# A row-variance kernel: the last row stored as four 128 B lines straight from the transpose, without closing barriers

## The chip, the cores and the metric

The kernel runs on one core of a Trainium2 chip. The metric is the device time of one execution in microseconds; lower is better. Positions in a trace are microseconds from the start of its span.

## The reference

```python
x = np.random.randn(8192, 8192).astype(np.float32)
def reference(x):
    return np.var(x, axis=1)        # 8192 variances
```

The input is 268 MB, the output 32 KB.

## The kernel before

SyncE streams the rows through three buffers; VectorE sums, ScalarE squares. The last two blocks are cut into pieces with a semaphore each, so that little work is left when the last one lands. What matters here is the end. The variances of the last 128 rows (called a row below, as they are one row of 128 outputs) come out of an aggregate as one column, are transposed in blocks of 32 x 32, and then lie as four lines of 32 values on partitions 0, 32, 64 and 96:

```python
        def variances(j, *marks):
            wait(v, *marks)
            ok = V.mark(v.bn_aggr(out=mv[j][:, 0:2], in_=st[j]))
            wait(v, ok)
            return V.mark(v.transpose(vl[j][:, 0:32], mv[j][:, 1:33]))
        ...
        ok = variances(1, done[1]["B"], done[1]["A"])
        wait(g, (V.sem, V.n - 1))
        g.sem_clear(range(own[0].num, own[-1].num + 1))
        final = []
        for b, (eng, copy) in enumerate(((v, v.tensor_copy), (a, a.copy), (g, g.tensor_copy)), 1):
            wait(eng, ok)
            moved = copy(out=vl[1][0:1, b * 32 : b * 32 + 32], in_=vl[1][b * 32 : b * 32 + 1, 0:32])
            final.append(moved.then_inc(gathered, 1).ins)
        ...                                                        # cut: three earlier stores
        final.append(store(out_r[r + 1 : r + 2], vl[1][0:1, :], (gathered, 3)).ins)
        sp.wait_ge(gathered, 3).then_inc(gathered, -3)
    tc.close()
    tc.compile()
    nc.sync.wait_ge(stored, 64).then_inc(stored, -64)
    ...                                                            # cut: closing barriers moved early
```

Three engines copy one line each beside the first, so that the row leaves as one line of 512 B. Two closing barriers of all engines and GpSimd's clear of the semaphores follow. The row before it, ready earlier, already leaves as four lines of 128 B.

## Time and profile before

| | before |
|---|---|
| time, median of the first four executions | 626.74 us (626.65 to 627.13) |
| span of the profiled execution | 625.66 us |
| share of the span in which the load queue is busy | 99.5% |
| last transpose starts | 624.057 |
| store of the last row issued | 624.572 to 624.799 |
| its semaphore complete, end of SyncE's wait | 625.629, 625.662 |

Read it from the end: the span ends with SyncE's wait for the last store. Everything from the transpose to there is one chain of 1.605 us; before the transpose VectorE works from 618.59 on with no pause over 35 ns, taking the last pieces about as they land; up to there the loads alone set the pace.

### The profile page before, as it was taken

Reading aid. Unit: us, or ns where it says so; the run is one execution under the profiler, and the core shown is the slowest. Engines: PE = TensorE matmul, PEld = TensorE weight load, DVE = VectorE, ACT = ScalarE, POOL = GpSimd, SP = SyncE. Lnnn points to the kernel's source line nnn. Section 1 sums busy time; section 2 is a strip of 40 time slices with the busy share of each in tenths; the row PEclk is TensorE's granted clock in tenths of the full one; section 3 lists DMA queues with packets and bytes.
Section 4 is the critical chain, followed back from the end, with each engine's and each line's share of the span. In section 5 each row is a group of like instructions: output and inputs, shape, how many; then the busy total and the mean of one; then the engine's idle time right before and its main releaser. Section 6 shows DMA issues by size and latency. Waiting matters only on the chain. (4 is left out here: it accounts for less than half of the span.)

```text
span 625.7 us, 990 instructions
## 1 busy us (share of the span) xinstructions
PE 0.6 (0%) x2; PEld 0.2 (0%) x2; DVE 292.1 (47%) x214; ACT 460.4 (74%) x166; POOL 1.6 (0%) x16
## 2 busy tenths in 40 slices
PE   0000000000000000000000000000000000000000
PEld 0000000000000000000000000000000000000000
DVE  0533455334554335543355533555334554345668
ACT  0566886668866688666796667976668866688698
POOL 0000000000000000000000000000000000000000
DMA  9999999999999999999999999999999999999997
GB/s 402 465 406 461 411 402 469 402 469 402 469 402 465 406 457 415 448 423 427 444 406 465 402 469 402 469 402 469 402 465 406 448 423 427 444 406 465 402 421 319
DMA packets 6121, 268.48 MB, mean 429 GB/s; under 512 B 712, under 2 KB 872, under 8 KB 1384
## 3 DMA queue, kind: packets, MB, share of 16 engines
q1 hardware_dynamic: 6120, 268.47, 99.5%
q14 instruction: 1, 0.01, 0.0%
HBM read 268.44 MB, written 0.03 MB: 429 GB/s over the span
## 5 line engine op out<-in xcount | busy, mean ns | idle before, releaser
L176 ACT ACTIVATE junk_a<-rows,means 128x8192 fp8e4 x30 | 213.7, 7122 | 160.7 <-ACTq L174 160.7
L100 DVE CUSTOM_DVE_ANT_0 junk_p<-rows 128x512 f32<-128x512 f32 (+4 forms) x63 | 145.8, 2314 | 325.8 <-DMA rows<-in_x_dram 325.8
L176 ACT ACTIVATE rows<-rows,means x30 | 213.2, 7106 | 0.0
L100 DVE CUSTOM_DVE_ANT_0 junk_s<-rows 128x4096 fp8e4<-128x4096 f32 (+3 forms) x34 | 139.1, 4093 | 5.5 <-DMA rows<-in_x_dram 5.5
L100 DVE DVE_READ_ACCUMULATOR2_ANT means<- 128x1 f32 x90 | 10.9, 121 | 0.0
L241 DVE BATCH_NORM_STATS2 st<-rows 128x6 f32<-128x512 f32 (+1 forms) x14 | 8.7, 672 | 1.0 <-DMA rows<-in_x_dram 1.0
L108 ACT ACTIVATE rows<-rows,st 128x3584 f32<-128x3584 f32 (+3 forms) x4 | 8.9, 2231 | 0.2 <-DVE st L100 0.2
L157 ACT ACTIVATE over<-means x30 | 8.4, 279 | 0.0
L108 ACT ACTIVATE rows<-rows,tmp 128x8192 f32<-128x8192 f32 x1 | 7.1, 7122 | 0.3 <-issue 0.3
L108 ACT ACTIVATE junk_a<-rows,tmp 128x8192 fp8e4<-128x8192 f32 x1 | 7.1, 7108 | 0.0
L176 ACT ACTIVATION_READ_ACCUMULATOR rows<-rows,means x30 | 5.6, 186 | 0.0
L176 ACT ACTIVATION_READ_ACCUMULATOR junk_a<-rows,means x30 | 5.6, 186 | 0.0
L169 ACT ACT_TABLE_LOAD x1 | 1.3, 1283 | 1.9 <-SPq L124 1.9
L214 POOL TENSOR_TENSOR ssq<-ssq,over 128x30 f32<-128x30 f32 x1 | 0.3, 251 | 596.3 <-ACT over L157 596.3
L221 PE MATMUL junk_p<-ident,ssq 128*31 128x128 f32 x2 | 0.6, 422 | 614.4 <-POOL ssq L216 614.4
L268 ACT COPY vl<-vl 1x32 f32<-1x32 f32 x1 | 0.2, 215 | 1.0 <-DVE vl L249 1.0
L247 DVE BATCH_NORM_AGGREGATE mv<-st 128x2 f32<-128x57 f32 (+1 forms) x2 | 0.7, 371 | 0.0
L108 ACT ACTIVATION_READ_ACCUMULATOR rows<-rows,st 128x1 f32 x4 | 0.8, 188 | 0.0
L249 DVE STREAM_TRANSPOSE vl<-mv 128x32 f32<-128x32 f32 x2 | 0.4, 211 | 0.1
L100 DVE DVE_READ_ACCUMULATOR2_ANT st<- 128x1 f32 x4 | 0.4, 112 | 0.0
L258 DVE TENSOR_SCALAR vs<-junk_p 31x256 f32<-31x256 f32 x1 | 0.4, 372 | 0.0
L221 PEld LDWEIGHTS junk_p<-ident,ssq 128*31 128x31 f32 x2 | 0.2, 140 | 614.4 <-POOL ssq L216 614.4
(17 smaller groups left out, 3.2 us busy)
## 6 DMA issues: line engine op xcount, KB each, us to landing
rows<-in_x_dram SPq DMA_DIRECT2D x2, 4096.0 KB, 37.4
rows<-in_x_dram SPq DMA_DIRECT2D x2, 1280.0 KB, 16.0
rows<-in_x_dram SPq DMA_DIRECT2D x1, 1792.0 KB, 11.9
rows<-in_x_dram SPq DMA_DIRECT2D x1, 1088.0 KB, 11.0
rows<-in_x_dram SPq DMA_DIRECT2D x1, 1024.0 KB, 25.5
rows<-in_x_dram SPq DMA_DIRECT2D x2, 512.0 KB, 12.3
rows<-in_x_dram SPq DMA_DIRECT2D x2, 256.0 KB, 13.1
rows<-in_x_dram SPq DMA_DIRECT2D x30, 42.3
```

What stands on the lines that cost most here:

```text
L100: ins = nc.vector.tensor_tensor_reduce(out=junk, in0=src[:, 0 : w // 2], in1=src[:, w // 2 : w], scale=scale, scalar=0.0, op0=ALU.add, op1 ...
L108: return A.mark(nc.scalar.activation(out=src if out is None else out, in_=src, func=ACTF.Square, bias=mean, scale=-1.0, accum_out=acc, **p ...
L157: return a.activation(out=out, in_=k, func=ACTF.Square, bias=rest, scale=root * (K / m - 1.0))
L169: a.activation(out=tmp[:, 7:8], in_=tmp[:, 6:7], func=ACTF.Square)
L176: a.activation(out=row if j else junk_a, in_=row, func=ACTF.Square, bias=about, scale=-1.0, accum_out=ssq[:, bass.ds(i * (J * SLOTS) + s * ...
L214: g.tensor_tensor(out=loop_rows, in0=loop_rows, in1=over[:, 0:t], op=ALU.subtract)
L221: t_ok = T.mark(nc.tensor.transpose(vp[:, j], ssq[:, j : r : J], ident))
L241: ok = V.mark(v.bn_stats(out=st[j][:, b : b + 6], in_=src[:, at : min(at + F, w)]))
L247: ok = V.mark(v.bn_aggr(out=mv[j][:, 0:2], in_=st[j]))
L249: return V.mark(v.transpose(vl[j][:, 0:32], mv[j][:, 1:33]))
L258: vs_ok = V.mark(v.tensor_scalar(out=vs.rearrange("t p j -> t j p"), in0=vp, scalar1=1.0 / m, scalar2=None, op0=ALU.mult))
L268: moved = copy(out=vl[1][0:1, b * 32 : b * 32 + 32], in_=vl[1][b * 32 : b * 32 + 1, 0:32])
```

## The change

Its intent: drop three copies and a wait from the chain, and drop the barriers. The core of the diff (the block that moved the barrier's instructions is cut):

```diff
-        wait(g, (V.sem, V.n - 1))
-        g.sem_clear(range(own[0].num, own[-1].num + 1))
-        for b, (eng, copy) in enumerate(((v, v.tensor_copy), (a, a.copy), (g, g.tensor_copy)), 1):
-            wait(eng, ok)
-            moved = copy(out=vl[1][0:1, b * 32 : b * 32 + 32], in_=vl[1][b * 32 : b * 32 + 1, 0:32])
-            final.append(moved.then_inc(gathered, 1).ins)
+        def lines_of(r):
+            return out_r[r].rearrange("(b k) -> b k", k=32)
-        final.append(store(out_r[r + 1 : r + 2], vl[1][0:1, :], (gathered, 3)).ins)
-        sp.wait_ge(gathered, 3).then_inc(gathered, -3)
+        store(lines_of(r + 1), vl[1][0::32, 0:32], ok)
...
+    for blk in (leave, end):
+        blk.instructions = [i for i in blk.instructions if isinstance(i, mybir.InstUnconditionalBranch)]
+    sp.sem_clear(range(own[0].num, section[0]["range_last"] + 1))
+    sp.wait_ge(stored, 64).then_inc(stored, -64)
```

More of the change, by code (lines that the diff above doesn't have):

```diff
@@ L77 @@
     vp = junk_p[0 : NT - 1, H - F : H - F + J * P].rearrange("t (j p) -> t j p", j=J)
-    stored, gathered = nc.alloc_semaphore("stored"), nc.alloc_semaphore("gathered")
+    stored = nc.alloc_semaphore("stored")
     own = [nc.alloc_semaphore(f"piece{i}") for i in range(J + len(ways[0]) + len(ways[1]))]
@@ L261 @@
         ok = variances(1, done[1]["B"], done[1]["A"])
-        wait(g, (V.sem, V.n - 1))
-        g.sem_clear(range(own[0].num, own[-1].num + 1))
-        final = []
-        for b, (eng, copy) in enumerate(((v, v.tensor_copy), (a, a.copy), (g, g.tensor_copy)), 1):
-            wait(eng, ok)
-            moved = copy(out=vl[1][0:1, b * 32 : b * 32 + 32], in_=vl[1][b * 32 : b * 32 + 1, 0:32])
-            final.append(moved.then_inc(gathered, 1).ins)
+        def lines_of(r):
+            return out_r[r].rearrange("(b k) -> b k", k=32)
         def store(dst, src, *marks):
@@ L274, in store @@
             return sp.dma_start(out=dst, in_=src).then_inc(stored, 16)
-        store(out_r[r].rearrange("(b k) -> b k", k=32), vl[0][0::32, 0:32], lines)
+        store(lines_of(r), vl[0][0::32, 0:32], lines)
         store(out_tj[0:16], vs[0:16], vs_ok)
         store(out_tj[16 : NT - 1], vs[16 : NT - 1])
-        final.append(store(out_r[r + 1 : r + 2], vl[1][0:1, :], (gathered, 3)).ins)
-        sp.wait_ge(gathered, 3).then_inc(gathered, -3)
+        store(lines_of(r + 1), vl[1][0::32, 0:32], ok)
     tc.close()
@@ L285 @@
     blocks = nc.main_func.blocks
-    nc.sync.wait_ge(stored, 64).then_inc(stored, -64)
     leave = next(blk for blk in blocks if "after_critical" in blk.name)
     end = next(blk for blk in blocks if blk.name.endswith("_end") and "tile_context" in blk.name)
-    arrive = [i for i in end.instructions if i.engine == sp.engine][:2]
-    end.instructions = [i for i in end.instructions if i not in arrive]
-    for ins in final:
-        inner = next(blk for blk in blocks if any(i.name == ins.name for i in blk.instructions))
-        off = [i for i in leave.instructions if i.engine == ins.engine
-               and not isinstance(i, mybir.InstUnconditionalBranch)]
-        leave.instructions = [i for i in leave.instructions if i not in off]
-        at = [i.name for i in inner.instructions].index(ins.name) - 1
-        if ins.engine == v.engine:
-            said = off[0].sync_info.on_update[0]
-            off = [v.sem_inc(SemaphoreHandle(said.ant_name, said.id)).ins]
-            for blk in blocks:
-                blk.instructions = [i for i in blk.instructions if i.name != off[0].name]
-            at = max(n for n, i in enumerate(inner.instructions) if isinstance(i, mybir.InstBNStats)) + 1
-        if ins.engine == sp.engine:
-            off += arrive
-        inner.instructions = inner.instructions[:at] + off + inner.instructions[at:]
+    section = [i.ant_dict for i in end.instructions if isinstance(i, mybir.InstISA)]
+    assert section[0]["range_first"] == own[-1].num + 1
+    for blk in (leave, end):
+        blk.instructions = [i for i in blk.instructions if isinstance(i, mybir.InstUnconditionalBranch)]
+    sp.sem_clear(range(own[0].num, section[0]["range_last"] + 1))
+    sp.wait_ge(stored, 64).then_inc(stored, -64)
     loads = []
```

## The prediction

> **What bounds the kernel now.** I read the page first, then its DMA part, then the timeline of the last microseconds and SyncE's own waits. From the page:
>
> ```profile
> span 625.7 us, 990 instructions
> PE 0.6 (0%) x2; PEld 0.2 (0%) x2; DVE 292.1 (47%) x214; ACT 460.4 (74%) x166; POOL 1.6 (0%) x16
> ...
> q1 hardware_dynamic: 6120, 268.47, 99.5%
> ...
> HBM read 268.44 MB, written 0.03 MB: 429 GB/s over the span
> ```
>
> One queue is busy 99.5% of the span; no engine is above 74%. The kernel is a stream of 268.44 MB, and its length is fixed by the transfers until the last piece lands. The change touches no load and no statistics, so all it can move is what follows the last piece. That part is in the timeline, whose columns are start, duration, engine, line, operation, tiles and count:
>
> ```profile
> 621.83 1.83 DVE L241 BATCH_NORM_STATS2 st<-rows 128x6 f32<-128x512 f32 x3
> ...
> 623.69 0.33 DVE L247 BATCH_NORM_AGGREGATE mv<-st 128x2 f32<-128x39 f32 x1
> 624.06 0.21 DVE L249 STREAM_TRANSPOSE vl<-mv 128x32 f32<-128x32 f32 x1
> 624.30 0.21 ACT L268 COPY vl<-vl 1x32 f32<-1x32 f32 x1 [1.02 <-DVE vl L249]
> 624.30 0.17 DVE L268 COPY vl<-vl 1x32 f32<-1x32 f32 x1
> 624.34 0.20 POOL L268 COPY vl<-vl 1x32 f32<-1x32 f32 x1 [9.98 <-DVE vl L249]
> 624.57 0.23 SPq L274 DMA_DIRECT2D out_dram<-vl  x1
> ```
>
> The reader is to see a strictly serial tail: statistics, aggregate, transpose, three copies side by side that bring four 32-wide lines into one partition, and the issue of the 512 B store. The span ends at 625.66, a microsecond after that issue. The individual records behind these views give the tail to the nanosecond: the transpose's semaphore is up at 624.280, the copies' three signals at 624.486, 624.526 and 624.555, the store issue runs 624.572 to 624.799, its only data packet starts at 625.275 and takes 27 ns, its completion mark starts at 625.299, the store's semaphore reaches its target at 625.629, and SyncE's wait for it runs 625.645 to 625.662. That wait is the end.
>
> The closing barriers, read by source line (engine, operation, count, durations in ns, first and last start):
>
> ```profile
> L284 SPq DRAIN  x3: 7/7/115, 624.3 to 625.0; - x3
> L284 POOLq DRAIN  x3: 34/82/279, 624.3 to 625.1; - x3
> L284 SPq EVENT_SEMAPHORE  x2: 17/17/17, 624.9 to 625.3; - x2
> L284 PEldq EVENT_SEMAPHORE  x2: 51/51/51, 624.8 to 625.3; - x2
> L284 POOLq EVENT_SEMAPHORE_RANGE_CLEAR  x1: 112/112/112, 624.9 to 624.9; - x1
> L286 SPq EVENT_SEMAPHORE  x1: 17/17/17, 625.6 to 625.6; - x1
> ```
>
> The last barrier instruction starts at 625.3 (its semaphore traffic stops at 625.347); the final wait is released at 625.645. The barriers are over about 0.30 us before the store has landed. The page's chain view ends in the barrier, at a GpSimd drain, because it does not follow the store; it must not be read as saying that the barrier sets the end.
>
> [...] 227 ns of issue, then 830 ns more until the semaphore (624.799 to 625.629). [...] the one-line store shows two updates, one at 625.025 and one at 625.629; the four-line store earlier shows one early update plus four. [...] the 128 B packets of the first store took 13 ns each[...]. [...] The trace shows semaphore clears from 625.997 to 626.656; all of it follows SyncE's end, so the measured time should move with SyncE's end.
>
> **The change part by part.**
>
> (1) The three copies go. The store may start from the transpose's own signal. SyncE started the earlier four-line store 17 ns after its signal (618.062 to 618.079), so the last store should start at 624.280 + 0.017 = 624.297 in place of 624.572: **-0.275 us**, all of it on the path.
>
> (2) The store changes from one line of 512 B to four of 128 B. Everything turns on this. By source line, min/median/max in ns:
>
> ```profile
> L274 SPq DMA_DIRECT2D out_dram<-vl x2: 227/433/639, 618.1 to 624.6; - x2
> L274 SPq DMA_DIRECT2D out_dram<-vs x2: 384/404/423, 618.8 to 619.2; - x2
> ```
>
> The 227 is the one-line store, the 639 the four-line store of the row before, exactly the form that the change now uses twice. If the length belongs to the form, the change adds 639 - 227 = **+0.412 us** on the path: net -0.275 + 0.412 = +0.137. If the 639 was a first-use cost (it is the kernel's first store to this output), the second of its kind should cost about what the one-line issue or a 128-line load issue after a wait costs (227 or 328): net -0.275 to -0.17. From the end of the issue to the landing I keep 830 ns[...].
>
> (3) The barriers and the drains go. They end 0.30 us before the landing, so they give 0. They would only have begun to matter if the landing came over 0.30 us earlier, and (1) asks for 0.275 at most. SyncE must keep them out of its way, though, and does: nothing stands between the store's issue and its wait but the clear.
>
> (4) SyncE now clears all the semaphores in one instruction behind the issue. GpSimd's clears took 96 ns for 12 semaphores and 112 ns for 14; 26 should take about 0.2 us, inside the 0.83 us of flight: 0. GpSimd's clear and its handshake between 624.06 and 624.24 went on beside the transpose: 0.
>
> Sum: -0.275 us with a cheap issue, +0.137 us with a dear one. From 626.69 that is 626.42 or 626.83.
>
> **The rivals.** First, *cheap issue*. For it: [...] the 15- and 16-line stores took only 423 and 384 back to back. Second, *dear issue*. For it: the same tile form, the same stride over partitions, and no other issue in the trace is over 440 ns, not even the first load. Also that someone put a 0.275 us gather ahead of a one-line store, which pays only if the four-line issue costs more than that. I give each about a half. Third, *the barrier was the bound*: the measured time includes the other engines' way out, so removing two barriers would let all of them leave early and save perhaps 0.5 us more. Against it: the landing is 0.30 us later than the last barrier signal, and the end needs SyncE. I give it one in twenty. Fourth, *small lines land late*: [...] Possible; it pushes up only.
>
> **Range and chances.** The mean of 626.42 and 626.83 is 626.6, which I predict: a change of less than 0.1 us, as the expectation over two outcomes that are 0.4 us apart. The runs of before span 626.65 to 627.13, and the profiled run was 627.12, so a median can be up to 0.45 us high by luck. Low end: 626.42 less 0.2 is 626.2. High end: 626.83 plus some of that scatter is 627.2. Two per cent is 12.5 us, fifty times anything here: within 2% has a chance of 0.99, the rest is shared.
>
> **What would show each step.** The last store's issue should start some 17 ns after the transpose's signal and within 0.25 us of the transpose's start; no copies after it. Its duration decides: near 230 to 330 (cheap) or near 640 (dear). From issue end to the landing about 0.83 us; more would be the small lines. No barrier instructions, and SyncE's clear done well before the landing. The load stream's length should agree to the scatter between runs. Wrong would be: a time under 626.1 (then the way out of the other engines counted), over 627.2 (then SyncE's clear or the small lines stand on the path), or a changed load stream.

Its sum: -0.275 us from (1) and 0 or +0.412 us from (2), 0 from (3) and (4), so -0.275 or +0.137 us, read against 626.69 as 626.42 or 626.83.

## The result, and the profile after

The changed kernel takes **628.18 us** (median of four, 628.03 to 628.27) against 626.74: slower by 1.44 us by the medians, ratio 1.0022 with a 95% interval of 1.0004 to 1.0039. A ratio is the mean time of one kernel's runs over that of the other's of the same rounds, so it is not quite the ratio of the medians quoted. The time lies outside the predicted range of 626.2 to 627.2.

From the page of the changed kernel:

```profile
span 626.9 us, 952 instructions
...
q1 hardware_dynamic: 6126, 268.47, 99.3%
q14 instruction: 1, 0.01, 0.0%
HBM read 268.44 MB, written 0.03 MB: 428 GB/s over the span
```

The stream is the same. Queue 14 moves one packet of program instructions; it has 0.0% of the time and matters below. Now the end of its timeline (start, duration, engine, line, operation, tiles):

```profile
623.64 0.33 DVE L247 BATCH_NORM_AGGREGATE mv<-st 128x2 f32<-128x39 f32 x1
624.00 0.21 DVE L249 STREAM_TRANSPOSE vl<-mv 128x32 f32<-128x32 f32 x1
624.24 0.54 SPq L268 DMA_DIRECT2D out_dram<-vl  x1
```

The stores, the clear and the final wait by source line (durations min/median/max in ns, first and last start):

```profile
L268 SPq DMA_DIRECT2D out_dram<-vl x2: 541/584/626, 618.0 to 624.2; - x2
...
L287 SPq EVENT_SEMAPHORE_RANGE_CLEAR  x1: 75/75/75, 624.8 to 624.8; - x1
...
L288 SPq EVENT_SEMAPHORE  x1: 17/17/17, 626.9 to 626.9; - x1
```

The copies are gone, the store starts at the transpose's heels, the clear takes 75 ns; yet the final wait ends at 626.9, 2.1 us after the issue's end. The DMA view of the window from 625.3 to 626.0 (the first line below has 40 slices of 17.5 ns) shows what ran meanwhile:

```profile
GB/s 0 0 0 0 468 0 7 8 8 0 0 0 0 0 0 0 0 0 0 0 0 0 0 0 0 0 0 0 0 0 0 0 0 0 8 0 0 0 0 0
DMA packets 9, 0.01 MB, mean 12 GB/s; under 512 B 8, under 2 KB 8, under 8 KB 8
...
q14 instruction: 1, 0.01, 4.6%
q1 hardware_dynamic: 8, 0.00, 0.7%
```

A packet's bytes are booked where it starts. The 468 is an 8 KB packet of instructions; 7, 8 and 8 are three lines of the store; the lone 8 is the fourth, half a microsecond later. The kernel before has the same packet (the 364 below, 624.521 to 624.995), but there it is over before the store's one line (the 23) leaves at 625.275. Its DMA view from 624.5 to 625.4, slices of 22.5 ns:

```profile
GB/s 364 0 0 0 0 0 0 0 0 0 0 0 0 0 0 0 0 0 0 0 0 0 0 0 0 0 0 0 0 0 0 0 0 0 23 0 0 0 0 0
...
q14 instruction: 1, 0.01, 3.3%
q1 hardware_dynamic: 2, 0.00, 0.2%
```

The individual records of the changed kernel (a completion mark is an update of the store's semaphore that the trace books to a DMA; the four after the fetch's start are put beside the four lines in order of time; SyncE's wait starts at 626.864, 0.016 us after the last):

```
        start    end      bytes  queue            completion mark lands
fetch   625.387  625.905  8192   14 instruction
line    625.422  625.433   128   1                625.768
line    625.436  625.447   128   1                625.776
line    625.450  625.461   128   1                625.809
line    625.901  625.914   128   1                626.848
```

The fourth line starts where the fetch ends, and its mark needs 0.95 us from its packet's start, where the others need 0.35. The balance from the transpose's start, before against after:

| part of the chain | before | after | difference |
|---|---|---|---|
| transpose's start to the issue | 0.515 | 0.239 | -0.276 |
| issue | 0.227 | 0.541 | +0.314 |
| end of the issue to the first packet | 0.476 | 0.639 | +0.163 |
| first packet to the landing of the row (after: of three lines) | 0.354 | 0.387 | +0.033 |
| the fourth line's landing after that | | 1.039 | +1.039 |
| landing to the end of SyncE's wait | 0.033 | 0.033 | 0 |
| sum | 1.605 | 2.878 | +1.273 |

After SyncE's end the traces show nothing but more semaphore updates (the way out), for 1.574 us before and 1.507 after. With the transpose 0.054 us earlier, 1.273 - 0.067 - 0.054 = 1.15 us, which is what the two profiled executions differ by (627.12 and 628.27). The profiled execution of before was the slowest of its four; the medians' further 0.3 us are scatter.

### The profile page after: what moved, and what is told of

The parts are those of the page before. It is cut to its first block, busy times and chain, and to the rows that moved or that the text cites. A ratio compares the mean times of both kernels' runs of the same rounds, so it can differ in the third digit from the quotient of the medians.

```text
span 626.9 us, 952 instructions
## 1 busy us (share of the span) xinstructions
PE 0.6 (0%) x2; PEld 0.2 (0%) x2; DVE 292.0 (47%) x213; ACT 460.1 (73%) x165; POOL 1.4 (0%) x15
```

## The experiments

Eighteen runs. The theory after the result, **F**: one line shares a DMA engine with an 8 KB fetch of program instructions, waits behind it, and has its mark held by it. It is read from the times of the records (line at 625.901, fetch until 625.905, mark 0.943 us later); the trace does not name DMA engines. Rivals: **S**, small lines land late by themselves; **W**, what is missing at the end (barriers, GpSimd's clear) costs the time. In the diffs `ready` and `lines` are marks that pass before the padded engine's next work on the data (`ready` at 3.02 us; VectorE's first sum starts at 21.9), so a wait on them costs only its place in the program. Waits are fused in pairs where they can be: 16 on SyncE or VectorE add 8 instructions to the trace.

### Whose fetch is it

**e1_pad_sync**: the changed kernel, and

```diff
+        for _ in range(16):
+            wait(sp, lines)
         store(lines_of(r + 1), vl[1][0::32, 0:32], ok)
```

> The changed kernel with 16 waits that are already satisfied added to SyncE's stream between the stores of the loop's rows and the last store, where SyncE idles for some 4.6 us. In the changed kernel one 8 KB packet of the instruction queue starts at 625.387 and ends at 625.905; three of the four 128 B lines start at 625.42 to 625.45 and land at 625.77 to 625.81, the fourth starts at 625.901 and lands at 626.848. Theory F (fetch collision): that packet is SyncE's own instruction fetch, started by its position in its stream; 16 more instructions bring it forward to about 620, so all four lines land by 625.8 to 625.9, the span is about 625.85 and the time about 1.0 us below the changed kernel's 628.2, near 626.8 to 627.1. Rival S (small lines): four parts of one 512 B block land late by themselves; the last landing stays near 626.8 and the time at 628.2. Rival W (way out): what is missing at the end costs the time; also 628.2.

Measured: 628.01 us against 626.86, ratio 1.0016. The fetch stayed behind the transpose (1.48 us after it), the fourth line landed at 627.436, 1.09 us after the third. My guess that the fetch is SyncE's fell; S and W are untouched by this run.

**e2_pad_others**: 16 waits on each of the other four engines.

```diff
         ready = G.mark(nc.gpsimd.memset(tmp, 0.0))
+        for _ in range(16):
+            for e in (nc.vector, nc.scalar, nc.tensor, nc.gpsimd):
+                wait(e, ready)
```

> Control: the changed kernel with 16 satisfied waits on each of VectorE, ScalarE, TensorE and GpSimd near the start, none on SyncE. If the fetch is SyncE's (theory F) it stays near 625.39 and the fourth line still lands near 626.85, time near 628.2. If the fetch belongs to one of the other four, it moves or goes, and the fourth line lands with the rest, time near 627.

Measured: the fetch moved to 619.791, and the four lines landed at 626.052, 626.075, 626.085 and 626.112. From the transpose to the end 1.835 us instead of 2.878. The late landing is gone with the same four small lines and without barriers: S and W fall as causes of that microsecond. The time was 627.48 us (one execution, state unknown) where near 627 was expected: part of the gain is missing, and e7 shows where it went.

**e7_pad_vector**: 16 waits on VectorE alone. **e8_pad_three**: 16 on ScalarE, TensorE and GpSimd, none on VectorE (same edit, other engines named).

> The changed kernel with 16 satisfied waits on VectorE alone, at the start of its stream. Sixteen on SyncE did not move the 8 KB fetch off the last store; sixteen on each of the other four engines moved it to 619.8 and the late line was gone. Theory V: the fetch is VectorE's, which in the changed kernel is the last of the four to reach the end (0.6 us before the fetch its arrival is signalled). Then here too the fetch starts near 619.8, all four lines land within 0.06 us of each other some 0.33 us after their packets, and from the transpose's start to the end of SyncE's last wait it takes about 1.83 us (changed kernel 2.88, before 1.61); time about 0.2 us above before. Rival: the fetch is another engine's; it stays within 1.5 us of the transpose, the fourth line lands about 1 us late, 2.9 us from the transpose.

> The complement: 16 satisfied waits on ScalarE, TensorE and GpSimd, none on VectorE. Theory V: nothing moves, the fetch starts some 1.4 us after the transpose, the fourth line lands about 1 us late, 2.9 us from the transpose's start to the end. Rival: fetch near 619.8, 1.83 us.

Measured: with VectorE padded the fetch starts at 619.813 and the chain is 1.839 us; with the other three padded it starts 1.37 us after the transpose, the fourth line lands 0.985 us after the third, and the chain is 2.814 us (627.69 us, one execution). The fetch is **VectorE's**. But e7 took 627.79 us against 626.76: the time did not come back. VectorE's timeline of e7, then of e8, shows why (in brackets: idle time before, and what ended it):

```profile
621.64 0.69 DVE L100 CUSTOM_DVE_ANT_0 junk_s<-rows 128x512 fp8e4<-128x512 f32 x1 [0.64 <-DMA rows<-in_x_dram]
```

```profile
620.63 0.69 DVE L100 CUSTOM_DVE_ANT_0 junk_s<-rows 128x512 fp8e4<-128x512 f32 x1
```

In e7 this sum waits 0.64 us for its piece. Fifteen of the piece's sixteen marks are there at 620.961, the last at 621.613; for the next two pieces the last is 0.675 and 0.600 us late. In e8 it is 0.105 behind, and in e7 itself it is 0.105 to 0.120 for the pieces that landed from 563 us up to the fetch. The page counts 16 DMA engines and a piece has sixteen marks; read as one mark from each, one DMA engine, from this the one that carried the fetch, lags to the end of the stream. From the store of the row before to the transpose it is 6.58 us instead of 5.99. So the fetch costs about 0.6 us in the stream and 1.0 us under the last store.

### The two parts of the change, each alone

**e3_one_line_no_barrier**: barriers gone, SyncE clears, but the row gathered and stored as one line.

```diff
+        for eng, copy, b in ((v, v.tensor_copy, 1), (a, a.copy, 2), (g, g.tensor_copy, 3)):
+            wait(eng, ok)
+            copy(out=vl[1][0:1, b * 32 : b * 32 + 32], in_=vl[1][b * 32 : b * 32 + 1, 0:32]).then_inc(gathered, 1)
-        store(lines_of(r + 1), vl[1][0::32, 0:32], ok)
+        store(out_r[r + 1 : r + 2], vl[1][0:1, :], (gathered, 3))
```

> The barrier part alone: no closing barriers, SyncE clears, but the last row is gathered by three copies and leaves as one line of 512 B as before. Theory F: issue starts near 624.57 and takes 0.23 us, the line lands near 625.63 as before; the barriers were hidden, so the span is 625.6 to 625.7; the time at most 0.1 us below before (626.6 to 626.7), unless the fetch is on the very DMA engine of the one line, which would add 0.5 to 1 us. Rival S: the same 626.6 to 626.7. Rival W (no barriers, or SyncE's clear, cost the time): near 628.

Measured: 627.00 us against 626.86, ratio 1.0001 (0.9988 to 1.0015); 1.650 us from the transpose to the end. Removing the barriers neither costs nor gains anything that can be told from the times.

**e4_four_lines_barrier**: the kernel before, barriers kept, but the store waits for the transpose only (SyncE's handshake instructions are placed around that wait so that it stays ordered before the clears; a first build without this was refused as a race). The copies still run, unused.

```diff
-        final.append(store(out_r[r + 1 : r + 2], vl[1][0:1, :], (gathered, 3)).ins)
+        final.append(store(out_r[r + 1].rearrange("(b k) -> b k", k=32), vl[1][0::32, 0:32], ok).ins)
-            off += arrive
+            off += [inner.instructions.pop(at)] + arrive
```

> The store part alone: barriers and GpSimd's clear kept as before, the last row leaves as four lines of 128 B from the transpose without waiting for the copies (which still run, their result unused). SyncE reaches the store near 624.37. Theory F: SyncE's stream is as long as before, the fetch stays near 624.5, before the lines; issue 0.54 us, landing about 0.98 us after its end, near 625.9; time 0.2 to 0.4 us above before, near 627.0. Rival S: the fourth line lands about 1.1 us later, near 627.0, time near 628.1. Rival W: no loss beyond the dear issue, near 627.0.

Measured: 627.26 us against 626.86, ratio 1.0005 (0.9991 to 1.0019); chain 2.150 us. SyncE's stores of e3, then of e4 (timeline):

```profile
624.15 0.23 SPq L272 DMA_DIRECT2D out_dram<-vl  x1
```

```profile
623.92 0.54 SPq L274 DMA_DIRECT2D out_dram<-vl  x1
```

In e4 the fetch ran from 624.312 to 624.619, ahead of the lines (625.09 to 625.16), so none queued behind it. Three marks land at 625.420 to 625.454; the fourth, whose packet was only 0.03 us behind, lands at 625.658, 1.04 us after the end of the fetch. That is the second half of theory F by itself: a mark comes late though the fetch is already over. That the fetch holds it is inferred from the times: in the runs with a clearly late mark (changed kernel, e1, e4, e8, e11, g6) it lands 0.90 to 1.04 us after the fetch's end. What it waits for in that time is not shown. In the kernel before and in e3 the one line's mark lands 0.634 and 0.545 us after it: not held, so by this reading its engine was another.

### Where the fetch costs nothing

**e9_pad48**: the changed kernel with 48 waits on VectorE; **e10_one_line_pad48**: the same on e3; **e11_changed_again**: the changed kernel unedited, on that chip.

> The changed kernel with 48 satisfied waits at the start of VectorE's stream in place of 16. With 16 the fetch left the store but struck VectorE itself: 0.64 us of idle before the 512-wide sum at 621.6 that the run with waits on the other three engines does not have, which ate the gain. Forty-eight should bring the fetch into VectorE's idle time before the last two blocks, at about 603 or earlier. Then neither stall nor collision: from the transpose's start to the end 1.84 us (changed kernel 2.88, before 1.61), no idle of 0.6 us in VectorE's tail, and the time about 1.04 below the changed kernel of the same chip, and 0.15 to 0.2 above before. If the sum is wrong (something else in the change costs), it stays 0.5 us or more above before.

> No barriers, SyncE clears, the row gathered and stored as one line as before, and the 48 waits on VectorE: the best of the parts. From the transpose's start to the end 1.61 to 1.65 us as before; the way out some 0.07 us shorter. Time equal to before or up to 0.1 us below it; if the fetch's place cost before anything, more.

> The changed kernel itself on the same chip as these, to compare within one chip: 1.2 to 1.5 us above before, 8 KB fetch 1.4 us after the transpose, fourth line landing about 1.0 us after the fetch's end, 2.88 us from the transpose to the end.

Measured, against 626.68: 627.66, 627.43 and 628.27 us (ratios 1.0013, 1.0012, 1.0018). The chains are 1.837, 1.614 and 2.773 us, as the theory wants. But in e9 the fetch ran at 596.999 in the stream, and the next piece's last mark came 0.521 us after its fifteenth, where it was 0.214 for the piece before the fetch; in e10 the two are 0.888 and 0.006. The lag stays to the end of the stream, 25 us later. VectorE's idle time was no refuge: by these late marks it is a DMA engine that is taken, not VectorE. Of the 0.94 us by which e9's chain is shorter than e11's, the means of the times show 0.43. My expectation for e9 and e10 failed there.

**f1_pad8**, **f2_pad11** (changed kernel) and **f3_one_line_pad8** (e3), same edit with 8, 11 and 8 waits:

> The changed kernel with 8 satisfied waits on VectorE. With 0 the 8 KB fetch meets the last store (1.2 us lost), with 16 and 48 it meets the load stream: its DMA engine then lands its share of every later piece 0.5 to 0.65 us after the other fifteen, which the tail waits for. Between the last load's landing (0.9 us before the transpose) and about 0.3 us after the transpose's start the fetch should cost nothing: stream as in the changed kernel (5.98 us from the first row's store to the transpose), 1.84 us from the transpose to the end, time 0.1 to 0.3 us above before. If 8 is too few, the fetch starts later and the fourth line's mark is held until about 1.0 us after the fetch's end.

> The same with 11 waits, for a fetch some tenths of a microsecond to two microseconds earlier than with 8. Free if it starts after the last load has landed; if it starts before, the last pieces' sixteenth mark is late by up to 0.6 us and the distance from the first row's store to the transpose grows from 5.98 towards 6.6.

> No barriers, SyncE clears, one gathered line, and 8 waits on VectorE: its fetch should fall between the load stream and the store. From transpose to end 1.61 to 1.65 us, stream undisturbed, the way out 0.07 us shorter than before: equal to before or up to 0.1 us below. This is the candidate to beat both kernels; not more than 0.1 us is expected of it.

Measured, against 626.73: 627.69, 627.66 and 627.55 us (ratios 1.0014, 1.0013, 1.0010). All three fetches started at 619.8 to 620.2, again in the stream, so these expectations failed as well: the last marks of the later pieces came 0.72 to 0.81 us after the fifteenth, and from the store of the row before to the transpose it was 6.68 to 6.73 us. The chains are 1.837, 1.845 and 1.613 us.

**g5_pad5** and **g6_pad6**, 5 and 6 waits:

```diff
         ready = G.mark(nc.gpsimd.memset(tmp, 0.0))
+        for _ in range(5):
+            for e in (nc.vector,):
+                wait(e, ready)
```

> The changed kernel with 5 satisfied waits on VectorE. With 8, 11 and 16 the fetch starts 4.4 to 4.7 us before the transpose, in the stream; the one-line version without barriers, 3 instructions longer, has it 0.75 us after the transpose; the changed kernel 1.4 us after. Five should put it between 1 us before and 0.5 us after the transpose. If it starts in the gap (from 0.9 us before to 0.3 us after the transpose): 5.98 us from the first row's store to the transpose, 1.84 from the transpose to the end, time 0.1 to 0.3 above before, 1 us below the changed kernel. If it starts up to 0.8 us after: the lines leave in time, and one mark comes about 1 us after the fetch's end, 2.0 to 2.2 us to the end.

> The same with 6 waits, some tenths of a microsecond earlier than with 5, by the same two readings; if it starts more than 0.9 us before the transpose, the distance from the first row's store to the transpose grows from 5.98 towards 6.6.

Measured: 626.97 and 627.12 us against 627.01, ratios 1.0001 (0.9988 to 1.0015) and 1.0002. The end of g5's timeline and its DMA view from 624.0 to 625.3 (slices of 32.5 ns):

```profile
623.76 0.21 DVE L252 STREAM_TRANSPOSE vl<-mv 128x32 f32<-128x32 f32 x1
624.00 0.54 SPq L271 DMA_DIRECT2D out_dram<-vl  x1
```

```profile
GB/s 0 0 0 0 252 0 0 0 0 0 0 0 0 0 0 0 0 0 0 0 0 0 0 0 0 0 0 0 0 0 0 0 0 0 0 0 8 4 4 0
...
q14 instruction: 1, 0.01, 2.4%
q1 hardware_dynamic: 8, 0.00, 0.4%
```

The fetch (the 252) now stands well ahead of the lines, after the loads: 624.162 to 624.655, lines from 625.178. The marks land at 625.512 to 625.565; chain 1.840 us; from the store of the row before to the transpose 6.003 us, so the stream is undisturbed. With the same small lines, the same missing barriers and five idle waits more (two instructions), the changed kernel is level with before. In g6 the fetch ends at 624.672 and one mark comes only at 625.710; chain 1.907 us. Two and three instructions more on VectorE (five and six waits) brought the fetch's start from 1.38 us after the transpose's to 0.40 and 0.53 after, four (eight waits) to 4.4 us before; I can't say why it jumps. This closes the account: without the collision the chain is 1.840 - 1.605 = 0.235 us longer than before, which the times cannot resolve, and with it 1.0 us more.

No version beat the kernel before measurably. g5 beats the changed kernel: its five times (626.86 to 627.25) all lie below those of e11 (627.66 to 628.41), on another chip whose before was no slower.

### What a store's issue costs, and a column

**e5_issue_forms** and **e12_issue_forms2** (e7 and e9 with the early stores split), **f4_issue_forms3** (f1, likewise); one execution each, of which only the lengths of the issues are read. The edit of e5 (the other two split the stores otherwise):

```diff
-        store(lines_of(r), vl[0][0::32, 0:32], lines)
+        store(lines_of(r)[0:2], vl[0][0:64:32, 0:32], lines)
+        store(lines_of(r)[2:4], vl[0][64:128:32, 0:32])
-        store(out_tj[16 : NT - 1], vs[16 : NT - 1])
+        for lo, hi in ((16, 24), (24, 28), (28, 30), (30, 31)):
+            store(out_tj[lo:hi], vs[lo:hi])
```

> What the issue costs by form, off the path: the first row's four lines leave as two stores of two lines (partitions 32 apart), the 31 rows of 1 KB as 16, 8, 4, 2 and 1 row, all right in value; with the 16 waits on VectorE. Known: 16 rows 384 ns, 15 rows 423 ns, 128 rows 328 to 432 ns, one line 227 ns after a wait, four lines 541 to 640 ns. Theory K (by the number of engines): the issue gets longer as fewer rows are served, by some 25 ns for each step from 16 down: 8 rows near 590, 4 rows near 690, 2 rows near 740 ns back to back[...]. Rival P (stride over partitions, or lines of 128 B): the 4 rows of 1 KB take no more than the 16, near 400, and the two-line stores as long as the four-line one. Rival C (first use): only the first store is long.

> Issue lengths by form again, with 48 waits on VectorE so that no fetch is near, in another order and with repeats: single lines of 128 B, two lines 32 partitions apart, then 4, 4, 8, 8, 4, 2 and 1 rows of 1 KB. The first such run gave 618 (two lines, first store), 493 (two lines), 388 (16 rows), 328 (8), 677 (4), 253 (2), 252 (1), 549 (four lines, last). If the length belongs to the form, the 4-row issues are all near 650 to 680, 8 rows near 330, 2 and 1 near 250, two lines near 490; if the 677 came from the fetch that ran just then or from a first use, the 4-row issues differ among themselves, the first being the longest or all near 350.

> Issue lengths once more, to part the stride over partitions from the length of a line: four lines of 128 B from adjacent partitions, four of 896 B adjacent, four of 128 B from every second partition, four of 896 B from every second, four of 1 KB from every second, 16 rows and 3 rows of 1 KB. So far four strided lines of 128 B took 540 to 560 ns (630 as the first store), 1 KB rows on adjacent partitions 250 to 300. If the stride is what costs: near 540 for the three strided ones and 300 for the adjacent ones. If the 128 B lines are what costs: near 540 for the two of 128 B only. If only the stride of 32 partitions costs: all near 300.

Measured issue lengths in ns, in order of issue:

```
e5   2x128B spaced 618, 493 | 16 rows 388 | 8 rows 328 | 4 rows 677 | 2 rows 253 | 1 row 252 | 4x128B spaced 549
e12  1x128B 322, 243 | 2x128B spaced 592 | 4 rows 403, 303 | 8 rows 296, 295 | 4 rows 295 | 2 rows 253 | 1 row 252 | 4x128B spaced 559
f4   4x128B spaced 658 | 4x128B adjacent 412 | 4x896B adjacent 279 | 4x128B spaced 647 | 4x896B spaced 732 | 4 rows spaced 577 | 16 rows 447 | 3 rows 283 | 4x128B spaced 549
```

("rows" are 1 KB on adjacent partitions; "spaced" is every 32nd partition for the variances' lines and every second otherwise.) The number of lines and their size hardly count: 243 to 303 ns for adjacent ones but for the first of a kind (322, 403, 412) and the stores of 8 rows (295 to 328) and 16 rows (388, 447). The same four lines of 128 B take 412 adjacent and 647 spaced, those of 896 B 279 and 732. Lines on partitions that are not neighbours cost 0.24 to 0.30 us more to issue (647 against 412; the 1 KB rows 577 against 279 to 303), and 0.45 in the pair of 279 and 732. The theory by number of engines, which asked for 590 ns for 8 rows and 740 for 2, fell (328 and 253 in e5). The first issue of a form was 0.08 to 0.13 us longer than a later one (e5: 618 against 493; e12: 322 against 243, 403 against 295 to 303; f4: 658 against 549). The 677 of e5 stays unexplained: four adjacent rows took 295 to 403 elsewhere, and the 8 KB fetch ran in that very time; the 732 of f4 had the fetch beside it too, so its 0.45 is not a clean size.

**e6_column**: on e7, the column straight from the aggregate, 128 lines of 4 B.

```diff
-        ok = variances(1, done[1]["B"], done[1]["A"])
+        wait(v, done[1]["B"], done[1]["A"])
+        ok = V.mark(v.bn_aggr(out=mv[1][:, 0:2], in_=st[1]))
-        store(lines_of(r + 1), vl[1][0::32, 0:32], ok)
+        store(out_r[r + 1].rearrange("(p o) -> p o", o=1), mv[1][:, 1:2], ok)
```

> A candidate to beat both: with the fetch moved off by the 16 waits on VectorE, the last row leaves as a column, 128 lines of 4 B straight from the aggregate, without transpose or copies. Issue should start about 0.36 us earlier than in the changed kernel, at the end of the aggregate, and take about 0.33 us as the 128-row loads do after a wait, with packets on all 16 engines. If 4 B lines land like the others (packets 0.5 to 0.65 us after the issue's end, marks 0.35 us later), it takes about 1.7 us from the aggregate's start to the end, against 1.97 in before (1.61 from the transpose plus 0.36): 0.25 us faster, plus 0.07 on the way out, near 0.3 us below before. [...]

Measured: 632.62 us against 626.76, ratio 1.0094, correct. Its timeline:

```profile
623.89 0.33 DVE L265 BATCH_NORM_AGGREGATE mv<-st 128x2 f32<-128x39 f32 x1
624.25 0.36 SPq L272 DMA_DIRECT2D out_dram<-mv  x1
```

The issue is as short as hoped (363 ns) and all packets are out by 625.3, but the sixteen marks land between 627.221 and 631.236, 1.9 to 5.9 us after that: 7.38 us from the aggregate's start to the end, where before took 1.97. Here small lines do land late, by themselves: what rival S says is so for 128 lines of 4 B (the reason is not shown), and not for four lines of 128 B, which in g5 land 0.33 to 0.34 us after their packets' starts, where the 512 B line of before took 0.354.

## Why the prediction was wrong

The measured 628.18 us lies above the range.

**Part (1), the earlier start: right.** -0.276 us measured, -0.275 predicted.

**Part (2), the form: the dear issue was right in kind, the size off.** The issue took 541 ns, so +0.314 instead of +0.412; the first store of the form carries a first-use part of 0.085 (626 against 541). The reason stood in the prediction only as one argument for the dear issue, "the same stride over partitions"; the issue runs, single executions, point to it: the lines' partitions are not neighbours. The cheap issue, given about a half, fell: first use is 0.085 of the 0.412.

**The step that failed** is "From the end of the issue to the landing I keep 830 ns". It took 2.065 us (624.783 to 626.848). In g5, without the collision, it takes 1.026 us: 0.196 more than 830 ns belongs to this form, and 1.039 to the fetch. The four lines were taken to land in the time of the one, but the fourth started at the fetch's end (625.901, where the third started at 625.450), and its mark came 0.943 us after that end: by theory F, its engine had another customer. The sign of it lay in the page that I read first: one packet of the instruction queue. I had its position in the records as well (624.521 to 624.995) and gave it no thought, because it cost nothing there. It lay between the last load and a store whose mark it did not delay (0.354 us from the packet). The change removed instructions from VectorE (269 in the trace where before has 275), and the fetch came 1.384 us after the transpose's start in place of 0.464; it also put out four lines, with four marks, in place of one, and one of them met it. Neither alone costs a microsecond: e3 has the one line, e4 the early fetch, and both are within 0.4 us of before.

**Part (3), the barriers: right.** They were hidden; e3 shows 1.650 us of chain without them. The third rival (0.5 us from the others' way out) is refuted: the way out was 1.574 us in before, 1.507 in the changed kernel, 1.440 in e4 with its barriers kept.

**Part (4), the clear: right.** 75 ns beside the flight, where about 0.2 us was expected.

**The fourth rival, small lines landing late,** pointed the right way, but small lines by themselves are not what happened: without the collision (g5) the four land 0.33 to 0.34 us after their packets' starts. Without the collision the sum is -0.276 + 0.314 + 0.196 = +0.234 us, the difference of g5's chain to that of before but for a nanosecond; in time the two are within the scatter (means 627.00 against 626.94). So with parts (1) and (2) and the form's 0.196 as measured the time stays inside the predicted range (g5: 626.97); the collision takes it out.

## What to carry to other kernels

Before changing the tail of a kernel, look at every other packet that moves near it, program fetches too: here the last completion mark came 1.04 us late beside a packet with 0.0% of the time. Adding or removing instructions on VectorE moved its fetch here (from 0.464 us after the transpose's start to 1.384 by the change, to 0.40 with five waits more); after such a change, look at where it has gone, and try a few idle instructions before judging the change itself (g5: 626.97 us where the changed kernel takes 628.18). In a tail, count a store's issue by whether its partitions are neighbours (here mostly 243 to 303 ns for one to four lines on adjacent partitions, 493 to 732 for two or four on partitions apart), and don't store very short lines into one row (128 lines of 4 B took 632.62 us against 626.76).
